# The new key and value of each sample written over the oldest row of its window while loading

## The chip, the cores and the metric

The kernel runs on one core of a Trainium2 chip. The metric is device microseconds (us) of one execution, the median of three runs; lower is better. TensorE is called PE in the rows, VectorE DVE, ScalarE ACT, GpSimd POOL and SyncE SP.

## What is computed

One step of a decoder trunk: a prompt of 512 tokens and eight samples of one new token each (`DEC_BATCH = 8`) go through a state-space head group and an attention head group, and then through one output projection. The change touches the sliding-window branch of the samples' attention. Each sample has a cache `cache_win` of the last 512 rows (a key and a value of 2 x 64 numbers each, 512 bytes), and its new token adds a 513th. The mask admits only 512 of them, so the oldest row drops out:

```python
WINDOW = 512
wrows = jnp.concatenate([cache_win[l], win_rows], axis=1)          # 513 rows
kwpos_s = past_len - win_buf + jnp.arange(win_buf + s_s)
wmask = (kwpos[None, :] <= qpos[:, None]) & (kwpos[None, :] > qpos[:, None] - WINDOW)
s = jnp.einsum('bqgrd,bwgd->bqgrw', q, kw) * scale
p = jax.nn.softmax(jnp.where(wmask[None, :, None, None, :], s, NEG_INF), axis=-1)
o_win = jnp.einsum('bqgrw,bwgd->bqgrd', p, vw)
```

The output also holds `win_sample`, the last 512 of the 513 rows.

## The kernel before

The samples are worked on in four pairs, counted 0 to 3 here. For a pair, `gather_pair` fetches the paged cache by indirect DMAs from GpSimd (tiles `kvg`, eight of 128 x 1024 numbers, 512 KB each), transposes and compresses it; `window_scores` then loads the window cache, keys into `wk` and values into `wv`, 128 partitions x 4 rows x 128 numbers for each sample, four loads in a pair, and makes the scores `Swn`; `finish_pair` does the three softmaxes, the products with the values and the gating. `finish_pair` of one pair is interleaved with `gather_pair` of the next. At the same time the prompt's attention and gated projection run: the generators `prompt` and `sample` are merged step by step, and a scheduler then sets the order of each engine. Each engine works through its own list strictly in that order.

The new token does not lie in `wk` and `wv`. `window_scores` sets the score of the oldest row (partition 0, row 0 of four) to `NEG` and adds one column, 256, for the new token, whose score `sample_setup` has made from `KN` into `snew`; `finish_pair` takes its probability out into `en`, spreads it in `pnw` over the eight samples, transposes it, and multiplies it with the new values in `kvs`:

```python
for b2 in range(2):
    for kd, t in enumerate((wk, wv)):
        nc.sync.dma_start(t[:, b2], cw[2 * pr_ + b2, :, kd].rearrange("(p r) g d -> p r (g d)", r=4))
```

`kvg`, `wk` and `wv` share four buffers (`ld`). Plain DMAs are issued from the lists of SP and ACT, and signal on eight semaphores, `DMAHW0` to `DMAHW7`, which the two engines' DMAs take in turn, in the order of the program. A DMA that takes a semaphore again has a wait in front of it for the DMA that had it before; this wait stands in the list of the engine that issues. On ACT, two such groups stand among the computing: the eight copies of `shift_window` (L1626, cache to `win_sample`, 511 KB each), four each beside two of the prompt's attention tiles, and the loads of `w_out` (L1563, L1567). On SP the transposed output of the state-space part (`yT`, four loads) and the gated projection's weights (`wg`, in halves) are loaded among the window loads.

Of the kernel before, what the change touches and what calls it, by code (L numbers as in the profile page):

```python
# [13 lines left out]
ALU = mybir.AluOpType  # L14
# [5 lines left out]
NEG = -1e30  # L20
# [16 lines left out]
def hymba_step_kernel(  # L37
# [8 lines left out]
    nc = tc.nc  # L46
    G, T = nc.gpsimd, nc.tensor
# [149 lines left out]
    p = pb("tr")  # L197
# [773 lines left out]
    for g in range(2):
        for b2 in range(2):
            V.tensor_copy(QB[64 * g:64 * g + 64, :, b2, 4 * g:4 * g + 4], qv[64 * g:64 * g + 64, :, b2, :])
    V.tensor_copy(KN.rearrange("p k b -> p (k b)"), p[:, 32:48])

    QT = [[ht("QT", 1024, F32R) for _ in range(2)] for _ in range(2)]
    KT = [[ht("KT", 1024, F32R) for _ in range(2)] for _ in range(2)]
# [294 lines left out]
            after_qk.append(lambda g=g, oT=oT: gated(g, oT))  # L1272


    snew = st([64, 8], "snew")
    gr3 = st([64, 4, 3], "gr3")
    idx = st([128, 8, 4], "idx", I32)
    ckv = cache_kv[0].rearrange("f (a j) k g d -> (f a) (j k g d)", j=2)
# [2 lines left out]
    def sample_setup():  # L1281

        pn = pb("cmp")
        for pr_ in range(4):
            for b2 in range(2):
                T.matmul(pn[32 * b2:32 * b2 + 32, 2 * pr_:2 * pr_ + 2], QB[:, pr_, b2, :], KN[:, :, 2 * pr_ + b2], start=True,
                         stop=True, skip_group_check=True, tile_position=(0, 32 * b2))
        V.tensor_copy(snew, pn[0:64, 0:8])
        pg = pb("cmp")
        for pr_ in range(4):  # L1290
            T.matmul(pg[0:64, 24 * pr_:24 * pr_ + 24], cst[:8, C_OHBT + 64 * pr_:C_OHBT + 64 * pr_ + 64], gates[:8, 4, :],
                     start=True, stop=True, skip_group_check=True)
        grow = k1("grow", 96, 64).rearrange("p (a k h) -> p a k h", k=3, h=8)
        V.tensor_tensor(grow, pg[0:64, 0:96].rearrange("p (a h k) -> p a k h", h=8, k=3),
                        cst[:64, C_OHH:C_OHH + 8].unsqueeze(1).unsqueeze(1).to_broadcast([64, 4, 3, 8]), op=ALU.mult)
        V.tensor_reduce(gr3, grow, axis=AX.X, op=ALU.add)

        with tc.issue_after(last["nr"].ins):
            for jq in range(4):
                V.tensor_scalar(idx[:, :, jq], pti, 64.0, cst[:, C_BASE:C_BASE + 1], op0=ALU.mult, op1=ALU.add)  # L1300
                if jq:
                    V.tensor_scalar(idx[:, :, jq], idx[:, :, jq], float(jq), None, op0=ALU.add)

        for kd in range(2):
            for n_ in ("h", "l"):
                XT[kd, n_] = st([128, 2, 258], "XT", F32R, tag="U", bufs=4)
                with tc.issue_after(last["nr"].ins):
                    V.memset(XT[kd, n_][:, :, 256:258].bitcast(F32), 0.0)

    def gather_pair(pr_, out):  # L1310
# [3 lines left out]
        Ssl = st([128, 513], "Ssl", bufs=2, tag="Ssl")  # L1314
        with tc.issue_after(last["nr"].ins):
            V.memset(Ssl[64:128, 512:513], NEG)
        V.tensor_copy(Ssl[0:64, 512:513], snew[:, 2 * pr_:2 * pr_ + 1])
        ph = pb("ph")
        ph3 = ph.rearrange("p (k n) -> p k n", k=2)
        kTs = []  # L1320
# [74 lines left out]
    def window_scores(pr_, out):  # L1395
        wk = ld("wk").rearrange("p (b r n) -> p b r n", b=2, r=4)
        wv = ld("wv").rearrange("p (b r n) -> p b r n", b=2, r=4)
        for b2 in range(2):
            for kd, t in enumerate((wk, wv)):
                nc.sync.dma_start(t[:, b2], cw[2 * pr_ + b2, :, kd].rearrange("(p r) g d -> p r (g d)", r=4))  # L1400
        Swn = st([128, 257], "Swn", bufs=1, tag="h0")
        kTs = []
        for b2 in range(2):
            p = pb("win")
            for r in range(4):
                T.transpose(p[:, 128 * r:128 * r + 128], wk[:, b2, r], ident)
            kT = k3("kT")
            S.copy(kT, p)
            kTs.append(kT)

        pw = pb("win")
        for a in range(2):
            for b2 in range(2):
                o = 64 * a + 32 * b2
                T.matmul(pw[o:o + 32, 0:256], QB[:, pr_, b2, :], kTs[b2][:, 256 * a:256 * a + 256], start=True, stop=True,
                         skip_group_check=True, tile_position=(0, o))
        V.tensor_copy(Swn[:, 0:256], pw[:, 0:256])
        V.memset(Swn[0:64, 0:1], NEG)
        V.memset(Swn[64:128, 256:257], NEG)
        V.tensor_copy(Swn[0:64, 256:257], snew[:, 2 * pr_ + 1:2 * pr_ + 2])  # L1420
        out[:] = [Swn, wv]
        yield 1

    def finish_pair(pr_, gat, win):
# [37 lines left out]
        for a in range(2):  # L1462
# [29 lines left out]
        V.tensor_copy(rden[:, 1:3], sm_[64:128])  # L1492
        V.tensor_tensor(rden[:, 1:3], rden[:, 1:3], sm_[0:64], op=ALU.add)

        en = st([64, 2], "en", bufs=2, tag="en")
        V.tensor_copy(en[:, 0:1], Ssl[0:64, 512:513])
        V.tensor_copy(en[:, 1:2], Swn[0:64, 256:257])
        rc = st([64, 3], "rc", bufs=2, tag="rc")
        V.reciprocal(rc, rden)
        V.tensor_tensor(rc, rc, gr3[:, pr_], op=ALU.mult)  # L1500
        V.tensor_tensor(en, en, rc[:, 1:3], op=ALU.mult)
        pnw_ = k1("pnw", 16, 64).rearrange("p (k b) -> p k b", k=2)
        V.tensor_tensor(pnw_, cst[:64, C_OHB + 8 * pr_:C_OHB + 8 * pr_ + 8].unsqueeze(1).to_broadcast([64, 2, 8]),
                        en.unsqueeze(2).to_broadcast([64, 2, 8]), op=ALU.mult)
# [253 lines left out]
```

## Time and profile before

| | us |
|---|---|
| median of three runs (467.05 to 469.04) | 468.19 |
| the profiled execution | 468.64 |
| its span, first to last instruction | 466.9 |
| PE busy | 452.1 |
| DVE busy | 348.8 |
| ACT busy | 241.3 |
| POOL busy | 95.4 |

The profile gives busy time by engine, a chain of waits followed back from the last instruction, times of single instructions on a timeline, and for chosen stretches the busy time of each engine with the granted clock of PE, the mean busy share of the core's 16 DMA engines and the GB/s they moved. Packets that overlap count twice in that share, so that it can come out over 1. A row with "q" behind the engine (SPq, ACTq) is the issue of a DMA in that engine's list. The moved bytes of one window load are 512 x 512 = 262,144.

### The profile page before, as it was taken

Reading aid. Unit: us, or ns where it says so; the run is one execution under the profiler, and the core shown is the slowest. Engines: PE = TensorE matmul, PEld = TensorE weight load, DVE = VectorE, ACT = ScalarE, POOL = GpSimd, SP = SyncE. Lnnn points to the kernel's source line nnn. Section 1 sums busy time; section 2 is a strip of 40 time slices with the busy share of each in tenths; the row PEclk is TensorE's granted clock in tenths of the full one; section 3 lists DMA queues with packets and bytes.
Section 4 is the critical chain, followed back from the end, with each engine's and each line's share of the span. In section 5 each row is a group of like instructions: output and inputs, shape, how many; then the busy total and the mean of one; then the engine's idle time right before and its main releaser. Section 6 shows DMA issues by size and latency. Waiting matters only on the chain.

```text
span 466.9 us, 10954 instructions
## 1 busy us (share of the span) xinstructions
PE 452.1 (97%) x4258; PEld 385.9 (83%) x4258; DVE 348.8 (75%) x942; ACT 241.3 (52%) x587; POOL 95.4 (20%) x104
## 2 busy tenths in 40 slices
PE   8999999999999998799999999999899999999996
PEld 4989999899999998698686776867568799799885
DVE  6978999998998998385676858687756687683332
ACT  5913764756324328475676668566856555342100
POOL 3100000056442000462342214321433010000000
PEclk9999999999999997789999999999999999999999
DMA  8776533614627433466143362429343784311211
GB/s 290 247 225 167 84 73 108 187 40 82 143 57 214 129 82 73 148 209 187 46 140 114 121 215 79 148 90 350 104 141 130 220 209 152 101 58 58 69 46 48
DMA packets 75635, 62.84 MB, mean 135 GB/s; under 512 B 29262, under 2 KB 69056, under 8 KB 75456
## 3 DMA queue, kind: packets, MB, share of 16 engines
q1 hardware_dynamic: 66208, 36.74, 28.2%
q0 software_dynamic: 4816, 17.03, 11.5%
q10 hardware_dynamic: 4560, 8.39, 5.7%
q8 instruction: 33, 0.54, 0.5%
q14 instruction: 18, 0.15, 0.1%
HBM read 55.63 MB, written 10.70 MB: 142 GB/s over the span
## 4 chain that ended last, share of the span: by engine, by line
PE 73%; DVE 13%; DMA 7%; POOL 3%; issue 2%; ACT 1%; SPq 0%; DVEq 0%; POOLq 0%; ACTq 0%
PE a L121 11%; PE a L122 11%; PE a L123 10%; PE ph L1372 8%; DMA kvg<-in_cache_kv_dram,idx 4%; PE a L1262 4%; PE t L1253 4%; PE a L1220 3%; PE t L1348 3%; PE c L1545 3%; POOL rsq L168 2%; DVE ga L62 2%; PE t L1338 2%; PE ph L473 1%; DMA x<-in_x_prompt_dram 1%
## 5 line engine op out<-in xcount | busy, mean ns | idle before, releaser
L121 PE MATMUL a<-hTh,whi 128*128 128x256 f32 (+1 forms) x192 | 54.8, 287 | 0.6 <-DVE sg L61 0.6
L122 PE MATMUL a<-hTh,wlo 128*128 128x256 f32 (+1 forms) x192 | 54.8, 287 | 0.0
L123 PE MATMUL a<-hTl,whi 128*128 128x256 f32 (+1 forms) x192 | 53.4, 284 | 0.0
L1329 POOL DMA_INDIRECT kvg<-in_cache_kv_dram,idx x32 | 32.8, 1026 | 82.2 <-PE c L1123 40.1
L168 POOL TENSOR_TENSOR rsq<-rsq,mhalf 128x6 f32<-128x6 f32 (+3 forms) x10 | 28.7, 2872 | 101.8 <-DVE rsq L62 101.8
L122 PE MATMUL a<-whi,hTl 128*128 128x256 f32 (+1 forms) x160 | 45.8, 287 | 0.0
L123 PE MATMUL a<-wlo,hTh 128*128 128x256 f32 (+1 forms) x160 | 45.3, 284 | 0.0
L121 PE MATMUL a<-whi,hTh 128*128 128x256 f32 (+1 forms) x160 | 45.2, 287 | 0.0
L1372 PE MATMUL ph<-XT,W1h 128*128 128x256 f32 x256 | 44.5, 298 | 0.0
L61 ACT ACTIVATE P<-a,mx 128x128 f32<-128x128 f32 (+3 forms) x64 | 33.6, 533 | 13.3 <-DVE mx L61 11.5
L61 DVE TENSOR_REDUCE mx<-a 128x1 f32<-128x384 f32 (+3 forms) x48 | 27.9, 596 | 13.8 <-PE a L1221 13.6
L121 PEld LDWEIGHTS a<-hTh,whi 128*128 128x128 f32 x192 | 36.2, 188 | 1.1 <-DVE sg L61 0.8
L122 PEld LDWEIGHTS a<-hTh,wlo 128*128 128x128 f32 x192 | 36.2, 188 | 0.9 <-issue 0.4
L122 PE MATMUL a<-woh,mixl 128*128 128x256 f32 x128 | 36.1, 283 | 0.0
L121 PE MATMUL a<-woh,mixh 128*128 128x256 f32 x128 | 36.1, 284 | 0.0
L123 PE MATMUL a<-wol,mixh 128*128 128x256 f32 x128 | 36.0, 283 | 0.0
L123 PEld LDWEIGHTS a<-hTl,whi 128*128 128x128 f32 x192 | 35.7, 189 | 0.1
L1372 PEld LDWEIGHTS ph<-XT,W1h 128*128 128x128 f32 x256 | 34.9, 192 | 0.3 <-ACT XT L61 0.2
L62 ACT CAST whi<-w 128x1024 fp32r<-128x1024 f32 (+4 forms) x26 | 23.9, 927 | 15.8 <-PE a L122 10.5
L61 ACT COPY pT<-t 128x512 f32<-128x512 f32 x40 | 23.1, 588 | 15.8 <-PE t L1253 12.6
L122 PEld LDWEIGHTS a<-whi,hTl 128*128 128x128 f32 x160 | 30.1, 188 | 1.2 <-issue 0.9
L121 PEld LDWEIGHTS a<-whi,hTh 128*128 128x128 f32 x160 | 29.9, 189 | 0.9 <-PE ph L473 0.4
(410 smaller groups left out, 1235.5 us busy)
## 6 DMA issues: line engine op xcount, KB each, us to landing
w<-in_w_in_dram SPq DMA_DIRECT2D x16, 512.0 KB
out_dram<-in_cache_win_dram ACTq DMA_DIRECT2D x8, 511.0 KB
x<-in_x_prompt_dram SPq DMA_DIRECT2D x4, 512.0 KB
TT<-scr_k SPq DMA_DIRECT2D x4, 512.0 KB
w<-in_w_in_dram SPq DMA_DIRECT2D x16, 128.0 KB
W1r<-in_cmp_w_dram SPq DMA_DIRECT2D x4, 512.0 KB
wk<-in_cache_win_dram SPq DMA_DIRECT2D x8, 256.0 KB
wv<-in_cache_win_dram SPq DMA_DIRECT2D x8, 256.0 KB
```

Source lines behind the costliest of these rows:

```text
L61: return f(*args, **kw)
L62: return f(*args, **kw)
L121: T.matmul(out, ah, bh, start=start, stop=False, skip_group_check=True)
L122: T.matmul(out, al, bh, start=False, stop=False, skip_group_check=True)
L123: T.matmul(out, ah, bl, start=False, stop=stop, skip_group_check=True)
L168: return G.tensor_tensor(out, out, mhalf[:parts, :cols], op=ALU.pow)
L1220: T.matmul(bank, QTv(g, r)[:, qsl], KTv(g, a)[:, brs, :n], start=(a == 0), stop=False, skip_group_check=True)
L1253: T.transpose(p[:, 128 * r:128 * r + 128], P[r][:, br, 128 * kt:128 * kt + 128], ident)
L1262: mm = T.matmul(po[64 * br:64 * br + 64, :], kvt[kt - 1][:, c0:c0 + 64], behind[kt - 1][br][0], start=(kt == 1), stop=(kt == i + 1), tile_ ...
L1329: G.indirect_dma_start(out=gt_, out_offset=None, in_=ckv, in_offset=bass.IndirectOffsetOnAxis(ap=idx[:, 2 * pr_ + b2, jq:jq + 1], axis=0))
L1348: T.transpose(p[:, 256 * g + 128 * b2:256 * g + 128 * b2 + 128], gts[jq][b2][:, o:o + 128], ident)
L1372: T.matmul(ph3[:, kd], (W1l if part == 1 else W1h)[kd][a][:, wsl], (xl if part == 2 else xh)[:, e, a:a + 256], start=(jq == 0 and kd == 0 ...
```

## The change

The new key and value go into `wk` and `wv` in place of the oldest row. Each of the four loads of a pair becomes three DMAs on SP: partitions 1 to 127 from the cache, rows 1 to 3 of partition 0 from the cache, and the new row from `kvs` (in SBUF) to row 0 of partition 0. `Swn` has 256 columns; the masked column, the extra column, the second half of `KN`, `snew`, `en` and `pnw`, and the second product with `kvs` are gone.

```diff
     def window_scores(pr_, out):
...
         for b2 in range(2):
+            b = 2 * pr_ + b2
             for kd, t in enumerate((wk, wv)):
-                nc.sync.dma_start(t[:, b2], cw[2 * pr_ + b2, :, kd].rearrange("(p r) g d -> p r (g d)", r=4))
-        Swn = st([128, 257], "Swn", bufs=1, tag="h0")
+                src = cw[b, :, kd].rearrange("(p r) g d -> p r (g d)", r=4)
+                nc.sync.dma_start(t[1:128, b2], src[1:128])
+                nc.sync.dma_start(t[0:1, b2, 1:4], src[0:1, 1:4])
+                nc.sync.dma_start(t[0:1, b2, 0], kvs[b:b + 1, 512 + 128 * kd:640 + 128 * kd])
+        Swn = st([128, 256], "Swn", bufs=1, tag="h0")
...
-        V.tensor_copy(Swn[:, 0:256], pw[:, 0:256])
-        V.memset(Swn[0:64, 0:1], NEG)
-        V.memset(Swn[64:128, 256:257], NEG)
-        V.tensor_copy(Swn[0:64, 256:257], snew[:, 2 * pr_ + 1:2 * pr_ + 2])
+        V.tensor_copy(Swn, pw[:, 0:256])
...
-        en = st([64, 2], "en", bufs=2, tag="en")
-        V.tensor_copy(en[:, 0:1], Ssl[0:64, 512:513])
-        V.tensor_copy(en[:, 1:2], Swn[0:64, 256:257])
+        en = st([64, 1], "en", bufs=2, tag="en")
...
-        V.tensor_tensor(en, en, rc[:, 1:3], op=ALU.mult)
+        V.tensor_tensor(en, Ssl[0:64, 512:513], rc[:, 1:2], op=ALU.mult)
...
-        for kd in range(2):
-            T.transpose(p[0:8, 320 + 64 * kd:384 + 64 * kd], pnw_[:, kd], i64)
+        T.transpose(p[0:8, 320:384], pnw_, i64)
...
-            for kd in range(2):
-                c0, o = 384 + 256 * kd, 320 + 64 * kd + 32 * b2
-                todo[2 * b2 + 1].append((pT1[0:8, o:o + 32], kvs[:, c0:c0 + 128]))
+            o = 320 + 32 * b2
+            todo[2 * b2 + 1].append((pT1[0:8, o:o + 32], kvs[:, 384:512]))
```

Three places in the order of the built programs follow: each row is line, operation, written tile, read tile, size, and the semaphores that it waits for.

On SP, before, the window loads of pair 0 (`wk_3499`, `wv_3500`) and of pair 1 (`wk_4234`, `wv_4235`):

```order
L1400 DMA wk_3499<-in_cache_win_dram 128x4x128 [waits DMASW1_49,DMASW5_49,DVE_49,DMAHW1_49,PE_49,Pool_49]
L1400 DMA wv_3500<-in_cache_win_dram 128x4x128 [waits DMASW2_49,DMASW6_49,DVE_49,DMAHW2_49,PE_49,Pool_49]
L1400 DMA wk_3499<-in_cache_win_dram 128x4x128 [waits DMAHW3_49]
L1400 DMA wv_3500<-in_cache_win_dram 128x4x128 [waits DMAHW4_49]
L1400 DMA wk_4234<-in_cache_win_dram 128x4x128 [waits DMASW7_49,DMAHW1_49,DMASW2_49,DMAHW3_49,DVE_49,DMAHW5_49,PE_49,Pool_49]
L1400 DMA wk_4234<-in_cache_win_dram 128x4x128 [waits DMAHW6_49]
L1400 DMA wv_4235<-in_cache_win_dram 128x4x128 [waits DMASW3_49,DMASW5_49,DMASW0_49,DMAHW7_49,DVE_49,PE_49]
L1400 DMA wv_4235<-in_cache_win_dram 128x4x128 [waits DMAHW0_49]
```

On SP, after, the loads of pair 1 alone (`wk_4233`, `wv_4234`):

```order
L1402 DMA wk_4233<-in_cache_win_dram 127x4x128 [waits DMAHW0_49,DMAHW1_49,DMASW7_49,DMAHW5_49,DMASW2_49,DMAHW7_49,DVE_49,PE_49]
L1403 DMA wk_4233<-in_cache_win_dram 1x3x128 [waits DMAHW6_49]
L1404 DMA wk_4233<-kvs 1x16x8
L1402 DMA wk_4233<-in_cache_win_dram 127x4x128
L1403 DMA wk_4233<-in_cache_win_dram 1x3x128
L1404 DMA wk_4233<-kvs 1x16x8 [waits DMAHW2_49]
L1402 DMA wv_4234<-in_cache_win_dram 127x4x128 [waits DMASW3_49,DMASW5_49,DMASW0_49,DMAHW3_49,DVE_49,PE_49]
L1403 DMA wv_4234<-in_cache_win_dram 1x3x128 [waits DMAHW4_49]
L1404 DMA wv_4234<-kvs 1x16x8 [waits DMAHW5_49]
L1402 DMA wv_4234<-in_cache_win_dram 127x4x128 [waits DMAHW7_49]
L1403 DMA wv_4234<-in_cache_win_dram 1x3x128 [waits DMAHW1_49]
L1404 DMA wv_4234<-kvs 1x16x8 [waits DMAHW3_49]
```

Four rows have become twelve, the size of the large one is 127x4x128 in place of 128x4x128, and the first eight of them take the semaphores DMAHW5, 6, 7, 0, 1, 2, 3 and 4.

On ACT, before, the first four copies of `shift_window`, which the scheduler puts beside pair 1:

```order
L61 COPY oT_4004<-a_3931 128x512 [waits PE_49]
L1626 DMA out_dram<-in_cache_win_dram 16x8176 [waits DMAHW1_49]
L61 CAST XT_2787<-t_3989 128x2x256 [waits PE_49]
L1626 DMA out_dram<-in_cache_win_dram 16x8176 [waits DMAHW2_49]
L61 CAST XT_2791<-t_4130 128x2x256 [waits PE_49]
L1626 DMA out_dram<-in_cache_win_dram 16x8176 [waits DMAHW3_49]
L61 ACTIVATE P_4042,den_4010<-a_4037,mx_4031 128x384 [waits DVE_49]
L61 COPY fT_3896<-c_3946 128x512 [waits PE_49]
L1626 DMA out_dram<-in_cache_win_dram 16x8176 [waits DMAHW4_49]
```

On ACT, after, the same four:

```order
L61 COPY oT_4006<-a_3933 128x512 [waits PE_49,Activation_49]
L1622 DMA out_dram<-in_cache_win_dram 16x8176 [waits DMAHW6_49]
L61 CAST XT_2786<-t_3991 128x2x256 [waits PE_49]
L1622 DMA out_dram<-in_cache_win_dram 16x8176 [waits DMAHW0_49]
L61 CAST XT_2790<-t_4129 128x2x256 [waits PE_49]
L61 COPY fT_3899<-c_4047 128x320 [waits PE_49]
L1622 DMA out_dram<-in_cache_win_dram 16x8176 [waits DMAHW2_49]
L61 ACTIVATE P_4044,den_4012<-a_4039,mx_4033 128x384 [waits DVE_49]
L61 ACTIVATE P_4073,den_4012<-a_4063,mx_4062 128x384 [waits DVE_49]
L1622 DMA out_dram<-in_cache_win_dram 16x8176 [waits DMAHW4_49]
```

Before, DMAHW1 to DMAHW4 had last been taken by the loads of pair 0. After, DMAHW6, 0, 2 and 4 have last been taken by rows 2, 4, 6 and 8 of the SP rows above, the loads of pair 1 itself.

On SP, before, from the values of pair 2 (`wv_4943`) to the first weights of the gated projection:

```order
L1400 DMA wv_4943<-in_cache_win_dram 128x4x128 x2
L1016 DMA yT_4851<-scr_y 128x520
L1016 DMA yT_4857<-scr_y 128x520
L1016 DMA yT_4861<-scr_y 128x520
L1016 DMA yT_4867<-scr_y 128x520
L1027 DMA wg_5176<-in_w_glu_dram 128x4x128 x2
```

On SP, after, the same stretch, with the waits:

```order
L1402 DMA wv_4942<-in_cache_win_dram 127x4x128 [waits DMASW3_49,DMASW4_49,DMASW1_49,DMASW5_49,DMASW0_49,DMASW6_49,DVE_49,DMAHW4_49,PE_49,Pool_49]
L1403 DMA wv_4942<-in_cache_win_dram 1x3x128 [waits DMAHW6_49]
L1404 DMA wv_4942<-kvs 1x16x8 [waits DMAHW0_49]
L1015 DMA yT_4850<-scr_y 128x520 [waits DMAHW2_49,PE_49,Activation_49]
L1015 DMA yT_4856<-scr_y 128x520 [waits DVE_49,PE_49,DMAHW3_49,Activation_49,Pool_49]
L1015 DMA yT_4860<-scr_y 128x520 [waits DMAHW4_49,PE_49,Activation_49]
L1015 DMA yT_4866<-scr_y 128x520 [waits DMAHW5_49,PE_49,Activation_49]
L1402 DMA wv_4942<-in_cache_win_dram 127x4x128 [waits DMAHW6_49]
```

The second load of these values now stands behind the `yT` loads, and the third `yT` load takes DMAHW4, which the first row here took. Beside pair 2 the four copies of ACT take DMAHW3, 5, 7 and 1 in the same way, the last of them behind the second load of `wk`. In pair 3 the `w_out` loads of ACT take semaphores of that pair's loads; the last that does so, the second half of `wo_6146`, takes the one of the last load of `wv`.

## Rows read from the trace of the kernel before

**Rows 1.** The page's head, and busy time, share and instructions by engine.

```profile
span 466.9 us, 10954 instructions
PE 452.1 (97%) x4258; PEld 385.9 (83%) x4258; DVE 348.8 (75%) x942; ACT 241.3 (52%) x587; POOL 95.4 (20%) x104
```

**Rows 2.** The page's chain that ended last, share of the span by engine.

```profile
PE 73%; DVE 13%; DMA 7%; POOL 3%; issue 2%; ACT 1%; SPq 0%; DVEq 0%; POOLq 0%; ACTq 0%
```

**Rows 3.** The page's DMA issues: out<-in, engine, count, KB each.

```profile
out_dram<-in_cache_win_dram ACTq DMA_DIRECT2D x8, 511.0 KB
...
wk<-in_cache_win_dram SPq DMA_DIRECT2D x8, 256.0 KB
```

**Rows 4.** Timeline of SP: start us, us, line, transfer; first issues of the four pairs.

```profile
210.44 0.62 SPq L1400 DMA_DIRECT2D wk<-in_cache_win_dram  x1
...
252.56 1.22 SPq L1400 DMA_DIRECT2D wk<-in_cache_win_dram  x2
...
307.10 1.21 SPq L1400 DMA_DIRECT2D wk<-in_cache_win_dram  x2
...
361.20 1.22 SPq L1400 DMA_DIRECT2D wk<-in_cache_win_dram  x2
```

**Rows 5.** Stretches: us, busy by engine (instructions), clock, DMA share, GB/s.

```profile
211.00:211.80 0.80, 0.80 (x9) 0.80 (x8) 0.80 (x2) 0.09 (x1) 0.40 (x1) 1.00 0.00 0
211.80:212.20 0.40, 0.40 (x6) 0.40 (x5) 0.40 (x3) 0.40 (x1) 0.00 (x0) 1.00 0.49 148
212.00:216.25 4.25, 4.25 (x38) 4.16 (x38) 3.75 (x10) 2.85 (x12) 0.24 (x1) 1.00 0.82 244
366.00:367.00 1.00, 1.00 (x11) 0.97 (x9) 0.93 (x3) 0.59 (x1) 0.39 (x1) 1.00 1.14 339
```

**Rows 6.** Timeline of PE: second transposes of the keys, pairs 0 and 1.

```profile
227.09 0.60 PE L1406 MATMUL c<-cst,wk 128*128 128x128 f32 x4
...
280.18 0.60 PE L1406 MATMUL c<-cst,wk 128*128 128x128 f32 x4
```

**Rows 7.** Timeline of ACT: copies, `yT` casts, a `wg` cast, `w_out` loads.

```profile
267.64 0.73 ACTq L1626 DMA_DIRECT2D out_dram<-in_cache_win_dram  x1
...
317.43 0.52 ACTq L1626 DMA_DIRECT2D out_dram<-in_cache_win_dram  x1
...
327.40 0.63 ACT L62 CAST yTh<-yT 128x520 fp32r<-128x520 f32 x1 [2.50 <-DMA yT<-scr_y]
...
328.09 1.28 ACT L62 CAST yTh<-yT 128x520 fp32r<-128x520 f32 x2
...
385.04 1.05 ACT L62 CAST wgh<-wg 128x1024 fp32r<-128x1024 f32 x1
...
393.91 1.30 ACTq L1567 DMA_DIRECT2D wo<-in_w_out_dram  x2
```

**Rows 8.** Timeline of POOL: two of the indirect loads.

```profile
252.87 0.98 POOL L1329 DMA_INDIRECT kvg<-in_cache_kv_dram,idx  x1 [3.85 <-DVE xr L62]
...
264.11 0.98 POOL L1329 DMA_INDIRECT kvg<-in_cache_kv_dram,idx  x1 [3.74 <-DVE rc L62]
```

**Rows 9.** One more stretch, columns as in the fifth group.

```profile
194.50:201.30 6.80, 5.06 (x30) 4.88 (x31) 3.30 (x8) 3.47 (x12) 4.46 (x6) 0.50 0.78 259
```

**Rows 10.** By tile or line: operation, count, ns min/median/max, first and last start.

```profile
L62 DVE MEMSET Swn<- x8: 59/59/59, 165.1 to 404.5; 64x1 f32 x8
L62 DVE COPY Swn<-snew x4: 135/146/146, 182.6 to 378.6; 64x1 f32<-64x1 f32 x4
L62 DVE COPY en<-Swn x4: 145/145/145, 262.5 to 421.5; 64x1 f32<-64x1 f32 x4
L1524 PE MATMUL c<-cst,pnw x8: 216/216/217, 271.4 to 427.2; 64*8 64x64 f32 x8
L1545 PE MATMUL c<-kvs,fT x32: 267/268/293, 275.4 to 432.8; 8*32 8x128 f32 x32
```

**Rows 11.** Timeline of PE: the products with the values of the last pair.

```profile
431.00 0.62 PE L1545 MATMUL c<-wv,fT 128*32 128x128 f32 x16
```

More of the change, by code (lines that the diff above doesn't have):

```diff
@@ L961, in hymba_step_kernel @@
     V.memset(QB, 0.0)
-    KN = st([128, 2, 8], "KN")
+    KN = st([128, 8], "KN")
     p = pb("tr")
@@ L967, in hymba_step_kernel @@
         T.transpose(p[:, 8 * r:8 * r + 8], qsv[:, r].rearrange("p g d -> p (g d)"), ident[:8, :8])
-    for kd in range(2):
-        T.transpose(p[:, 32 + 8 * kd:40 + 8 * kd], kvs[:, 256 * (kd + 1):256 * (kd + 1) + 128], ident[:8, :8])
+    T.transpose(p[:, 32:40], kvs[:, 256:384], ident[:8, :8])
     qv = p[:, 0:32].rearrange("p (r a b) -> p a b r", r=4, b=2)
@@ L973, in hymba_step_kernel @@
             V.tensor_copy(QB[64 * g:64 * g + 64, :, b2, 4 * g:4 * g + 4], qv[64 * g:64 * g + 64, :, b2, :])
-    V.tensor_copy(KN.rearrange("p k b -> p (k b)"), p[:, 32:48])
+    V.tensor_copy(KN, p[:, 32:40])
     QT = [[ht("QT", 1024, F32R) for _ in range(2)] for _ in range(2)]
@@ L1272, in attention @@
             after_qk.append(lambda g=g, oT=oT: gated(g, oT))
-    snew = st([64, 8], "snew")
+    snew = st([64, 4], "snew")
     gr3 = st([64, 4, 3], "gr3")
@@ L1285, in sample_setup @@
             for b2 in range(2):
-                T.matmul(pn[32 * b2:32 * b2 + 32, 2 * pr_:2 * pr_ + 2], QB[:, pr_, b2, :], KN[:, :, 2 * pr_ + b2], start=True,
+                T.matmul(pn[32 * b2:32 * b2 + 32, pr_:pr_ + 1], QB[:, pr_, b2, :], KN[:, 2 * pr_ + b2:2 * pr_ + b2 + 1], start=True,
                          stop=True, skip_group_check=True, tile_position=(0, 32 * b2))
-        V.tensor_copy(snew, pn[0:64, 0:8])
+        V.tensor_copy(snew, pn[0:64, 0:4])
         pg = pb("cmp")
@@ L1316, in gather_pair @@
             V.memset(Ssl[64:128, 512:513], NEG)
-        V.tensor_copy(Ssl[0:64, 512:513], snew[:, 2 * pr_:2 * pr_ + 1])
+        V.tensor_copy(Ssl[0:64, 512:513], snew[:, pr_:pr_ + 1])
         ph = pb("ph")
@@ L1500, in finish_pair @@
         V.tensor_tensor(rc, rc, gr3[:, pr_], op=ALU.mult)
-        V.tensor_tensor(en, en, rc[:, 1:3], op=ALU.mult)
-        pnw_ = k1("pnw", 16, 64).rearrange("p (k b) -> p k b", k=2)
-        V.tensor_tensor(pnw_, cst[:64, C_OHB + 8 * pr_:C_OHB + 8 * pr_ + 8].unsqueeze(1).to_broadcast([64, 2, 8]),
-                        en.unsqueeze(2).to_broadcast([64, 2, 8]), op=ALU.mult)
+        V.tensor_tensor(en, Ssl[0:64, 512:513], rc[:, 1:2], op=ALU.mult)
+        pnw_ = k1("pnw", 8, 64)
+        V.tensor_scalar(pnw_, cst[:64, C_OHB + 8 * pr_:C_OHB + 8 * pr_ + 8], en, None, op0=ALU.mult)
         V.tensor_scalar(Pc2, Pc2, rc[:, 0:1], None, op0=ALU.mult)
@@ L1508, in finish_pair @@
         V.tensor_scalar(Ssl[:, 0:512], Ssl[:, 0:512], sm_[:, 0:1], None, op0=ALU.mult)
-        S.mul(Swn[:, 0:256], Swn[:, 0:256], sm_[:, 1:2])
+        S.mul(Swn, Swn, sm_[:, 1:2])
         i64 = ident[:64, :64]
@@ L1522, in finish_pair @@
         T.transpose(p[:, 256:320], Pc2, i64)
-        for kd in range(2):
-            T.transpose(p[0:8, 320 + 64 * kd:384 + 64 * kd], pnw_[:, kd], i64)
+        T.transpose(p[0:8, 320:384], pnw_, i64)
         S.copy(pT1[:, 0:320], p[:, 0:320])
-        V.tensor_copy(pT1[0:8, 320:448], p[0:8, 320:448])
+        V.tensor_copy(pT1[0:8, 320:384], p[0:8, 320:384])
         yield 1
@@ L1538, in finish_pair @@
             todo[2 * b2].append((pT1[:, 256 + 32 * b2:288 + 32 * b2], vc))
-            for kd in range(2):
-                c0, o = 384 + 256 * kd, 320 + 64 * kd + 32 * b2
-                todo[2 * b2 + 1].append((pT1[0:8, o:o + 32], kvs[:, c0:c0 + 128]))
-        for j in range(8):
+            o = 320 + 32 * b2
+            todo[2 * b2 + 1].append((pT1[0:8, o:o + 32], kvs[:, 384:512]))
+        for j in range(7):
             for q in range(4):
```

## The prediction

> **What bounds the kernel now.** I read the page's head and busy line first [rows 1]: PE is busy 452.1 of 466.9 us, 97%, so it has almost no idle time in which a late transfer could hide, and any stop of PE shows in the span nearly whole. The chain of waits says the same [rows 2]: PE 73%, DVE 13%, DMA 7%. Then I looked for the slack of the work that changes. The list of DMA issues gives eight loads of `wk`, and as many of `wv`, at 256 KB, and eight copies of 511 KB from ACT [rows 3]. SP issues the first load of the pairs at 210.44, 252.56, 307.10 and 361.20 [rows 4]. In pair 0 PE transposes the second half of the keys, which is the third load of the pair, from 227.09 on [rows 6]: these loads now have 16.65 us from issue to use and never hold PE.
>
> **The new loads: how many engines carry one.** In the order of the built program other transfers stand in 16 equal parts: a copy of 511 rows is 16x8176, one key row is 1x16x8. The large load stands as 127x4x128, and 127 has no divisor but 1. So either it goes whole to one of the 16 DMA engines, or the engines share it as they share 128 rows. I take the first, because the cut into 16 parts has a purpose only if transfers are dealt out by equal parts of their outer dimension; no row of this trace shows such a load.
>
> A rule bears on this. The Trainium skill ("DMA: Bandwidth & Descriptors", section "Why a DMA increments its semaphore by 16 and not by 1") says that a DMA from SP or ACT uses the largest number of engines up to 16 that divides the slowest dimension of both sides, and gives 127 partitions as an example of one engine; by it the sum is the 597 below, without it about 468. No run here shows it yet.
>
> **Price of one load.** It moves 127 x 4 x 512 = 260,096 bytes. The fastest stretch I found moves 339 GB/s over 16 engines, 21.2 each; while the four loads of pair 0 run, 244 GB/s at a share of 0.82, so 244 / (0.82 x 16) = 18.6 for a busy engine [rows 5]. That gives 12.3 to 14.0 us, and I take 13.1 (19.9 GB/s). Spread, it would take about 260,096 / 339 GB/s = 0.8 us; that is the other end. The same page, section "Specifications", states about 27 GiB/s for an engine; by it a load would take 9.0 us and the sum below would be about 544, an estimate from a figure that the stretches above don't reach.
>
> Two smaller prices belong to it. First bytes move about 1.4 us after an issue (210.44 to 211.8: no bytes until then, 148 GB/s after) [rows 4, 5]. And every other transfer puts a sixteenth on the same engine, at 19.9 GB/s 1.64 us for 512 KB and 0.82 for 256 KB. The 1x3x128 and 1x16x8 pieces move 1.5 KB and 512 bytes; I set them at nothing. The eight further issues of a pair cost SP 0.61 us each [rows 4], 4.9 us, which lies under the 13.1 us of the load before; if the loads were spread, the third load would be issued four issues, 2.5 us, later, and the cushion of 16.65 us still covers that.
>
> **Who waits.** Four loads are now 52 us on one engine, and what waits differs by pair. I go through them; "late" is against the trace of before, and adds up, since nothing in PE's list can run ahead of a stopped transpose for long.
>
> Pair 0. PE wants the third load at 227.1. It ends at 210.4 + 1.4 + 3 x 13.1 + 3.3 (two indirect loads of 512 KB that fall beside, as at 252.87 [rows 8]) = 254.4. Late: 27.3. The engine is free of the fourth at 267.5.
>
> Pair 1. First issue 252.6 + 27.3 = 279.9, so the backlog is gone. PE itself would wait for the second load of `wk`, but ACT is stopped sooner: by the order, its fourth copy of `shift_window` waits for DMAHW4, which now belongs to the 1x3x128 piece behind the third large load (it belonged to pair 0 before), and everything behind it in ACT's list (casts, exponentials, PSUM copies) that PE needs waits too. Before, that copy was issued at 267.64 [rows 7]. Now the load ends at 279.9 + 1.4 + 39.3 + 3.3 + 3 x 1.64 (the three copies ahead) = 328.8. Late: 61.2. Engine free at 343.5.
>
> Pair 2. First issue 307.1 + 61.2 = 368.3. The fourth copy, at 317.43 before [rows 7], here waits for the second `wk` load: 402.4 against 378.6. Then the third `yT` load, which stands on SP behind the third large load and takes its DMAHW4, waits for that: 368.3 + 1.4 + 39.3 + 3.3 + 6.6 (four copies) = 418.9, and lands some 2.2 us later (1.4 and 0.8 for 266 KB), 421.1. Its cast on ACT began at about 328.75 (the second of the two from 328.09 [rows 7]; the first, at 327.40, had waited 2.50 us for its `yT`, so there is no slack). Late: 92.4.
>
> Pair 3. First issue 361.2 + 92.4 = 453.6. The `w_out` loads on ACT wait for this pair's loads in turn, the last of them for the fourth: 453.6 + 1.4 + 4 x 13.1 + 1.6 (a gather) + 3.3 (four halves of `wg`) + 9.8 (`w_out` loads: six of 256, three of 512 KB) = 522.1. It was issued at about 394.6 (second of the two from 393.91 [rows 7]). Late: 127.5.
>
> **The sum.** 466.9 + 127.5 = 594.4. Three small terms. After a long stop PE may run at half clock for a while: 6.8 us at a granted 0.50 stand in the trace once [rows 9], which costs 3.4; after four stops 0 to +14, I take +7, half. PE can work ahead of ACT at the last stop, whose products with the values come at 431.0, well behind 394.6 [rows 7, 11]: 0 to -13, I take -5. The removed work: four transposes of 216 ns, sixteen products that pipeline like those with the values (0.62 us for sixteen [rows 11]; 268 ns is their latency), eight memsets of 59, and four copies each of 146 and 145 ns [rows 10], together 0.9 + 0.6 + 0.5 + 1.2 = 3.2 us if all were on the path; most DVE work has slack, so -1 (0 to -3.2). Span 595.4; the execution is 1.7 us longer than the span now (468.64 against 466.9), so **597 us**. The profiled time is 0.1% from the median, and I leave it there. Everything but the price of a load is small: it enters 13 times (3 + 3 + 3 + 4), so 12.3 or 14.0 us make 587 or 609, and the small terms widen that to about 570 to 622. As the price is of a case no row shows, I reach further: 540 is a price of 8.7 us, 650 one of 17.2.
>
> **Rivals.**
>
> Spread after all: the large load is shared by the engines, takes under 1 us as today, and the whole change is three more small DMAs behind each and the removed work: 468, bounds -3 to +2. For it: the trace of before shows only spread loads, at 244 GB/s [rows 5]. Against it: the cut into 16 elsewhere.
>
> ACT is not held: loads on one engine, but ACT's waits for the shared semaphores end with the small pieces or earlier ones, and only true readers wait. Pair 0 as above, 27.3. Pair 1: second `wk` load at 279.9 + 1.4 + 26.2 + 1.6 + 6.6 = 315.7 against 280.18 [rows 6], 35.5. Pair 2: the `yT` load as above, from an issue of max(307.1 + 35.5, 343.6): 393.2, landed 395.4, 66.7. Pair 3: issue 427.9, the last half of `wg` at 460.4 against 385.04 + 66.7 = 451.7 [rows 7], 75.4; the last load of `wv` is in by 496, before 431.0 + 75.4 [rows 11]. Together 466.9 + 75.4 + 1.7 + some 1 = 545. For it: no row shows which of two waits on ACT ends last. Against it: the order names the semaphores, and a list is worked through strictly in order.
>
> Faster: loads spread or hidden, and the removed work all on the path: 3.2 us of PE's and DVE's chain, 465.5. It decides only if over 2.3 us of the 3.2 count, and DVE, with 348.8 of 466.9 busy [rows 1], has slack over most of the span.
>
> **How the numbers follow.** One engine with all stops: 0.82. One engine with ACT free: 0.07. Spread, no difference: 0.07. Faster: 0.04. A measurement of this kernel tells about 0.5% from no change, so faster 0.04, same 0.07, slower 0.89. The range 540 to 650 takes in the main case with its price from 8.7 to 17.2 us and the second rival; about 0.15 stays outside, nearly all of it at 468 and below.
>
> **What would show it.** In the changed kernel's trace: from the first issue of a pair, a stretch of about 50 us with a DMA share near 1/16 and about 20 GB/s, where the four loads took 4.25 us before; PE idle by about 27 us before the second key transposes of pair 0; ACT idle in front of a copy of `shift_window` in pair 1 and of the `w_out` loads in pair 3, and before a `yT` cast in pair 2; SP's issues in a run of twelve. If the first stretch shows 200 GB/s or more, the forecast is wrong at its first step. If it shows 20 GB/s and the time is near 545, the waits on ACT are the wrong step; if the stops are where I put them with other lengths, the price is.

## The result, and the profile after

The changed kernel takes 589.45 us (median of six runs, 584.69 to 590.76) against 468.66 for the kernel before in the same comparison: 1.257 times as long, 95% interval 1.253 to 1.261. The forecast was 597, with 540 to 650 as its range.

The page of the kernel after: its head, busy time by engine, and the chain of waits by engine and by line, to be read against [rows 1, 2].

```profile
span 586.9 us, 10944 instructions
PE 477.5 (81%) x4237; PEld 402.7 (69%) x4237; DVE 346.8 (59%) x922; ACT 241.2 (41%) x587; POOL 93.9 (16%) x104
...
PE 44%; SPq 24%; DMA 16%; DVE 10%; issue 2%; POOL 2%; ACT 1%; ACTq 0%; POOLq 0%; DVEq 0%
```

The span is 120.0 us longer. PE falls from 97% to 81% busy, and a quarter of the chain that ended last is now SP issuing DMAs, which had 0% before [rows 2].

The same view as in [rows 5] (busy by engine, PE clock, DMA share, GB/s), between the second and the fourth load of pair 0:

```profile
228.50:252.00 23.50, 2.88 (x12) 2.10 (x10) 2.62 (x7) 0.81 (x4) 0.76 (x1) 0.57 0.07 22
...
238.00:248.00 10.00, 0.00 (x0) 0.00 (x0) 0.00 (x0) 0.00 (x0) 0.00 (x0) 0.50 0.07 22
```

This is the stretch that the prediction asked for first. The DMA share is 0.07, about one engine of 16, at 22 GB/s, where the four loads had moved at 244 [rows 5]. The trace's packets of 512 bytes, one for each row, pass one after the other, about 43 in a microsecond. In the ten microseconds from 238 on no engine computes at all.

SP's timeline of pair 0 (start us, us, line, transfer), the first issues of the three other pairs, the held issue and the `yT` loads of pair 2, and the last load of pair 3, beside [rows 4]:

```profile
209.68 0.74 SPq L1402 DMA_DIRECT2D wk<-in_cache_win_dram  x1
210.47 13.88 SPq L1403 DMA_DIRECT2D wk<-in_cache_win_dram  x1
224.40 0.60 SPq L1404 DMA_DIRECT2D wk<-kvs  x1
225.24 0.71 SPq L1402 DMA_DIRECT2D wv<-in_cache_win_dram  x1
226.00 10.69 SPq L1403 DMA_DIRECT2D wv<-in_cache_win_dram  x1
...
237.33 0.69 SPq L1402 DMA_DIRECT2D wk<-in_cache_win_dram  x1
238.06 10.56 SPq L1403 DMA_DIRECT2D wk<-in_cache_win_dram  x1
...
280.39 0.68 SPq L1402 DMA_DIRECT2D wk<-in_cache_win_dram  x1
...
362.91 0.68 SPq L1402 DMA_DIRECT2D wk<-in_cache_win_dram  x1
...
393.95 11.46 SPq L1403 DMA_DIRECT2D wv<-in_cache_win_dram  x1
...
406.13 4.00 SPq L1015 DMA_DIRECT2D yT<-scr_y  x4
...
445.43 0.72 SPq L1402 DMA_DIRECT2D wk<-in_cache_win_dram  x1
...
494.41 0.69 SPq L1402 DMA_DIRECT2D wv<-in_cache_win_dram  x1
495.14 16.66 SPq L1403 DMA_DIRECT2D wv<-in_cache_win_dram  x1
```

One thing here was not foreseen: the issue behind a large load (L1403, the 1x3x128 piece) takes 10.56 to 16.66 us, where an issue took 0.62 before [rows 4]. SP is held until about three quarters of the large load have gone. More on that in the last section.

PE and ACT at the places where the prediction put the four stops (start, duration, and in brackets the idle time before and what ended it); before, they are [rows 6, 7]:

```profile
252.23 1.09 PE L1410 MATMUL c<-cst,wk 128*128 128x128 f32 x4 [20.85 <-DMA wk<-kvs]
...
311.74 0.59 ACT L61 CAST XT<-t 128x512 fp32r<-128x512 f32 x1 [13.99 <-DMA wk<-in_cache_win_dram]
...
327.14 0.52 ACTq L1622 DMA_DIRECT2D out_dram<-in_cache_win_dram  x1
327.70 0.58 ACT L61 ACTIVATE P<-a,mx 128x384 f32<-128x384 f32 x1 [13.92 <-DMA wv<-in_cache_win_dram]
...
411.04 1.30 ACT L62 CAST yTh<-yT 128x520 fp32r<-128x520 f32 x2 [8.71 <-DMA yT<-scr_y]
412.40 1.26 ACT L62 CAST yTh<-yT 128x520 fp32r<-128x520 f32 x2
...
515.58 0.66 ACTq L1563 DMA_DIRECT2D wo<-in_w_out_dram  x1
516.29 0.63 ACT L62 ACTIVATE gx<-gx 128x512 f32<-128x512 f32 x1 [5.36 <-DMA wv<-in_cache_win_dram]
```

In pair 0 PE waits 20.85 us for the third load (and 3.30 for the first); what lands last of it is the new row, which SP could issue only behind the held issue. In pair 1 it is ACT: the operation at 327.70 neither reads nor writes `wv`, yet the view gives a `wv` load as what ended the idle time. Between the two stands the fourth copy of `shift_window`, and that is what waited, for the semaphore that the 1x3x128 piece behind the third large load had taken. In pair 2 ACT waits before the first `yT` cast, in pair 3 in front of the `w_out` loads.

### The profile page after: what moved, and what is told of

The parts are those of the page before. It is cut to its first block, busy times and chain, and to the rows that moved or that the text cites. A ratio compares the mean times of both kernels' runs of the same rounds, so it can differ in the third digit from the quotient of the medians.

```text
span 586.9 us, 10944 instructions
## 1 busy us (share of the span) xinstructions
PE 477.5 (81%) x4237; PEld 402.7 (69%) x4237; DVE 346.8 (59%) x922; ACT 241.2 (41%) x587; POOL 93.9 (16%) x104
## 4 chain that ended last, share of the span: by engine, by line
PE 44%; SPq 24%; DMA 16%; DVE 10%; issue 2%; POOL 2%; ACT 1%; ACTq 0%; POOLq 0%; DVEq 0%
SPq L1403 21%; PE a L121 7%; PE a L122 7%; PE a L123 7%; DMA wv<-in_cache_win_dram 7%; DMA wk<-in_cache_win_dram 3%; PE ph L1371 3%; PE a L1261 2%; PE a L1219 2%; POOL rsq L168 2%; PE t L1252 2%; DMA kvg<-in_cache_kv_dram,idx 2%; DVE ga L62 1%; PE t L1347 1%; SPq L1402 1%
## 5 line engine op out<-in xcount | busy, mean ns | idle before, releaser
L1371 PE MATMUL ph<-XT,W1h 128*128 128x256 f32 x256 | 50.3, 324 | 22.6 <-ACT XT L61 22.6
L61 DVE TENSOR_TENSOR XT<-t,XT 128x512 fp32r<-128x512 f32 x32 | 21.9, 686 | 62.3 <-ACT XT L61 62.2
L1371 PEld LDWEIGHTS ph<-XT,W1h 128*128 128x128 f32 x256 | 39.3, 214 | 24.4 <-ACT XT L61 23.7
L1219 PE MATMUL a<-KT,QT 128*128 128x512 f32 (+2 forms) x96 | 31.9, 431 | 15.7 <-ACT P L61 15.7
L61 ACT CAST XT<-t 128x512 fp32r<-128x512 f32 x32 | 18.6, 589 | 52.4 <-DMA wk<-in_cache_win_dram 26.7
```

Of the source, the lines that this page charges most:

```text
L61: return f(*args, **kw)
L1219: T.matmul(bank, QTv(g, r)[:, qsl], KTv(g, a)[:, brs, :n], start=(a == 0), stop=False, skip_group_check=True)
L1371: T.matmul(ph3[:, kd], (W1l if part == 1 else W1h)[kd][a][:, wsl], (xl if part == 2 else xh)[:, e, a:a + 256], start=(jq == 0 and kd == 0 ...
```

## The experiments

Each is one edit of the kernel after (of the kernel before in `e2_before_split`). The question was which part of the change costs the 121 us, whether it is the count of partitions, and whether the stops hang on semaphores.

**The 127-partition piece alone, in the kernel before** (`e2_before_split`):

```diff
-                nc.sync.dma_start(t[:, b2], cw[2 * pr_ + b2, :, kd].rearrange("(p r) g d -> p r (g d)", r=4))
+                src = cw[2 * pr_ + b2, :, kd].rearrange("(p r) g d -> p r (g d)", r=4)
+                nc.sync.dma_start(t[1:128, b2], src[1:128])
+                nc.sync.dma_start(t[0:1, b2], src[0:1])
```

> The kernel before with one part of the change alone: each window load is split into partitions 1 to 127 and partition 0, both from the cache; the extra score column, mask and second product stay, and no new row is written. Theory: all of the loss comes from the 127-partition piece: 560 to 592, four loads of 11.5 to 13 us in a row at about 22 GB/s in each pair. As eight DMAs per pair in place of twelve share the eight semaphores otherwise, the stop of pair 1 is some 12 us shorter (ACT's last copy waits for the second load), that of pair 2 some 12 us longer (the yT loads stand behind four). Rival (the cost sits in the new row out of SBUF, or in the taken-out work): 466 to 472.

Measured: 589.39 us, ratio 1.257 (1.253 to 1.261), as slow as the whole change. Its window row during pair 0, ACT's last copy of the first four, and the `yT` casts:

```profile
232.00:250.00 18.00, 1.24 (x4) 0.55 (x3) 2.20 (x6) 0.81 (x4) 0.77 (x1) 0.50 0.07 22
...
314.38 1.16 ACTq L1628 DMA_DIRECT2D out_dram<-in_cache_win_dram  x2
...
421.87 1.28 ACT L62 CAST yTh<-yT 128x520 fp32r<-128x520 f32 x2 [21.13 <-DMA yT<-scr_y]
423.22 0.63 ACT L62 CAST yTh<-yT 128x520 fp32r<-128x520 f32 x1
```

Again 22 GB/s at a share of 0.07. Pair 1 begins at 283.08 here, so ACT's stop ends some 32 us after the first issue (the last of the two issues from 314.38; 46.8 in the kernel after); pair 2 begins at 361.51, and the third `yT` cast, at 423.22, comes 62 us later (49.5). That is the shift of about a load each way that the semaphores and SP's order gave. The new row and the removed work have no part in the loss. This kernel still has one DMA more for each load than the kernel before; whether that counts, the third experiment shows.

**All 128 partitions, and the new row written over the old one** (`e1_full_then_row`):

```diff
-                nc.sync.dma_start(t[1:128, b2], src[1:128])
-                nc.sync.dma_start(t[0:1, b2, 1:4], src[0:1, 1:4])
-                nc.sync.dma_start(t[0:1, b2, 0], kvs[b:b + 1, 512 + 128 * kd:640 + 128 * kd])
+                nc.sync.dma_start(t[:, b2], src)
+        for b2 in range(2):
+            b = 2 * pr_ + b2
+            for kd, t in enumerate((wk, wv)):
+                nc.sync.dma_start(t[0:1, b2, 0], kvs[b:b + 1, 512 + 128 * kd:640 + 128 * kd])
```

> The changed kernel, but each load takes all 128 partitions x 4 rows from the cache again (four DMAs), and four DMAs of one row each then write the new key and value over the oldest row. Theory (one DMA engine carries the 127-partition load): with 128 partitions the loads are as short as before, the overwriting rows wait for them inside the 16.65 us cushion, and only the removed work is left: 465.5 to 468.5, 0 to 3 us under before; DMA at over 200 GB/s behind a pair's first issue. Rival (the new row itself, its DMAs and the waits between load and row, are the cost): still well over 500, since the rows are written here too and now wait for the load.

Measured: 467.76 us, ratio 0.999 (0.996 to 1.002). The window row behind the first issue of pair 0 (208.14 in this trace):

```profile
211.00:213.00 2.00, 2.00 (x20) 2.00 (x18) 1.81 (x5) 1.60 (x7) 0.00 (x0) 1.00 1.00 300
```

300 GB/s with PE busy throughout, and the whole loss is gone. The waits of the new rows for the loads lie in the cushion.

**127 cut into 112 and 15** (`e3_112_15`, and `e11_112_15_again`, the same kernel measured again):

```diff
-                nc.sync.dma_start(t[1:128, b2], src[1:128])
+                nc.sync.dma_start(t[1:113, b2], src[1:113])
+                nc.sync.dma_start(t[113:128, b2], src[113:128])
```

> The changed kernel with the 127 partitions cut into 112 (1 to 112) and 15 (113 to 127), both beginning off partition 0 as before the cut; sixteen DMAs per pair. Theory (the engines used are given by a divisor of the partitions): 112 goes to 16 engines and 15 to 15, and a pair's loads take 4 to 6 us: 464 to 472. Rival (a load that begins at partition 1, or that leaves out a row, is what is slow): as the changed kernel, 575 to 592. Rival (twelve or sixteen issues per pair on SP are the cost): as slow or slower than the changed kernel.

> e3_112_15 once more (112 and 15 partitions, no DMA waits for another one's data), beside e10 and e12. Theory: 465 to 468, ratio to before 0.994 to 1.000 as the first time. Rival (the first difference was noise): 468 to 469.5.

Measured: 466.98 us, ratio 0.997 (0.994 to 0.9995), and again 467.07 us, 0.997 (0.995 to 0.999). The window row over the first load of 112 partitions in pair 0 of `e3_112_15`:

```profile
211.10:211.60 0.50, 0.50 (x7) 0.46 (x6) 0.50 (x3) 0.12 (x1) 0.00 (x0) 1.00 0.99 298
```

All sixteen engines are busy. The same rows go to the same places from the same odd starting partition, with four more DMAs in a pair, and nothing is lost. Neither the start at partition 1 nor the issues on SP is the cause; the count 127 is. The piece of 15 also tells which rule holds: by the largest power of two in the count, 127, 122 and 112 would fall on one, two and sixteen engines too, but 15 on one. Its 60 packets pass in about half a microsecond, up to 23 in a tenth of one, where one engine passes about 43 in a whole one: 15 goes to several engines, as the divisor says.

**127 cut into 122 and 5** (`e4_122_5`; the diff is that above with 123 in place of 113):

> The changed kernel with the 127 partitions cut into 122 (2 x 61) and 5. Theory (largest divisor up to 16): 122 goes to two engines, 5 to five; a load takes 122 x 2048 / 2 bytes at 21 to 22 GB/s, about 5.8 us, and DMA runs at 40 to 45 GB/s in the stretch where the changed kernel showed 22. The stops shrink from 120 us to some 25 (third load of pair 0 about 231 against 227.1, then +9, +6 and +6): 478 to 505. Rival (only multiples of 16 or 8 are spread, everything else goes to one engine): 560 to 590 and 22 GB/s. Rival (one engine only for a prime count): 464 to 472.

Measured: 511.46 us, ratio 1.092 (1.089 to 1.096). Its window row in pair 0, and SP from the third load to the fourth:

```profile
226.00:232.00 6.00, 0.10 (x1) 0.00 (x0) 2.12 (x6) 0.53 (x4) 0.76 (x1) 0.94 0.13 40
...
225.17 0.71 SPq L1402 DMA_DIRECT2D wk<-in_cache_win_dram  x1
225.92 4.22 SPq L1403 DMA_DIRECT2D wk<-in_cache_win_dram  x1
230.19 0.69 SPq L1404 DMA_DIRECT2D wk<-in_cache_win_dram  x1
230.93 0.58 SPq L1405 DMA_DIRECT2D wk<-kvs  x1
231.56 0.70 SPq L1402 DMA_DIRECT2D wv<-in_cache_win_dram  x1
```

The share is 0.13, two engines of 16, at 40 GB/s: so the large load does go to as many engines as the divisor says. The time was 6 us above what I had given for it. From one large load to the next SP needs 6.4 us (225.17 to 231.56: the held issue and three more in line), not the 5.8 of the bytes alone; that the stops add this up to the 6 us is my reading and was not tested.

**A quarter of each load on 127 partitions** (`e9_quarter_on_127`):

```diff
-                nc.sync.dma_start(t[1:128, b2], src[1:128])
-                nc.sync.dma_start(t[0:1, b2, 1:4], src[0:1, 1:4])
+                nc.sync.dma_start(t[:, b2, 1:4], src[:, 1:4])
+                nc.sync.dma_start(t[1:128, b2, 0], src[1:128, 0])
```

> The changed kernel with a quarter of each load on 127 partitions: rows 1 to 3 of all 128 partitions in one DMA, row 0 of partitions 1 to 127 in a second, the new row in a third; the semaphores fall as in the changed kernel, twelve DMAs per pair. Theory (one engine for the 127): 127 x 512 bytes at 21.5 GB/s are 3.0 us, with the large part some 3.6 us a load; third load of pair 0 about 222 against 227.1, no stop; third load of pair 1 some 20 us after the first issue where 15 were free, so a stop of 2 to 6; little after: 468 to 478. Next issue on SP held for less than 2 us. Rival (a fixed price of each 127-partition DMA or of the new row, whatever its size): 560 and more.

Measured: 478.15 us, ratio 1.021 (1.013 to 1.028), just over the upper edge. SP's third load of pair 0 to the fourth, PE's second key transposes, and ACT's fourth copy:

```profile
217.53 0.59 SPq L1402 DMA_DIRECT2D wk<-in_cache_win_dram  x1
218.16 0.36 SPq L1403 DMA_DIRECT2D wk<-in_cache_win_dram  x1
218.57 3.63 SPq L1404 DMA_DIRECT2D wk<-kvs  x1
222.24 0.59 SPq L1402 DMA_DIRECT2D wv<-in_cache_win_dram  x1
...
228.21 0.60 PE L1410 MATMUL c<-cst,wk 128*128 128x128 f32 x4
...
273.22 0.52 ACTq L1622 DMA_DIRECT2D out_dram<-in_cache_win_dram  x1
```

The price falls with the bytes: with a quarter of them on one engine, 4.7 us from load to load beside indirect loads, PE does not wait in pair 0, and ACT's copy comes 5.6 us later than before [rows 7] instead of 59.5. Two per cent remain; I read them as shorter stops of the same kind (two `yT` casts of pair 2 wait 2.68 and 2.27 us, where one had waited 2.50 [rows 7]). Of the 9.7 us of span, 7.2 lie between the first issues of pairs 2 and 3; what makes them up was not tested. SP's issue was held longer than the 2 us I had expected.

**The same DMAs in another order** (`e7_small_first`): the 1x3x128 piece and the new row ahead of the 127 partitions.

> The changed kernel with each load's three DMAs in another order: the 1x3x128 piece, the new row, then the 127 partitions. Every transfer and every reader is the same; what moves is which DMA has which semaphore. Theory (ACT and SP are stopped by semaphores that the loads have taken): ACT's fourth copy in pair 1 now waits for the row ahead of the third large load, so that stop falls from 46.8 us after the pair's first issue to some 30 (two loads), the last w_out load waits for three loads in place of four, and the other two stops stay: 550 to 572. Rival (only the readers of the loaded tiles and the queue of the one engine count): as the changed kernel, 583 to 592.

Measured: 574.01 us, ratio 1.227 (1.218 to 1.236), two microseconds over my range. ACT at the fourth copy of pair 1 (whose first issue is at 280.86), and at the last `w_out` load that waits for pair 3 (first issue 443.22):

```profile
314.89 0.58 ACT L61 ACTIVATE P<-a,mx 128x384 f32<-128x384 f32 x1 [16.04 <-DMA wk<-in_cache_win_dram]
315.00 0.52 ACTq L1622 DMA_DIRECT2D out_dram<-in_cache_win_dram  x1
...
500.46 0.61 ACTq L1563 DMA_DIRECT2D wo<-in_w_out_dram  x1
```

The two stops are 34.1 and 57.2 us long, where the kernel after has 46.8 and 70.2: each about one load shorter, though every transfer and every reader is the same. So ACT was held by semaphores, which the rival "ACT is not held" denied. Of these 25.5 us only 15 show in the time: from the end of the stop in pair 1 to the next first issue (358.65) it is now 43.7 us, 35.8 in the kernel after, where 19 of the matmuls of that stretch had run during the longer stop.

**The large DMAs issued by GpSimd** (`e6_large_from_pool`: `nc.gpsimd` in place of `nc.sync` in the line of the 127 partitions).

> The changed kernel with only the 127-partition DMAs issued by GpSimd, the other two of a load by SP. The semaphores of SP and ACT are then no longer taken by the large loads. Theory in the sharper form of the Trainium skill (page DMA: Bandwidth & Descriptors, section Why a DMA increments its semaphore by 16 and not by 1: GpSimd's direct copies may be cut into ceil(partitions / 16) per engine): loads on all engines, over 150 GB/s behind the first issue, 465 to 475, with POOL's list a few us busier. Rival (one engine whoever issues): about 22 GB/s, pair 0 as late as in the changed kernel, the semaphore stops gone, GpSimd's indirect loads behind the window loads on that engine: 540 to 580.

Measured: 584.80 us, ratio 1.251 (1.242 to 1.260). Its window rows while one load moves and while mostly two do, POOL's issue of one, and PE behind it:

```profile
228.00:232.00 4.00, 4.00 (x35) 3.82 (x36) 1.92 (x5) 3.58 (x16) 2.97 (x1) 1.00 0.08 23
...
238.00:244.00 6.00, 0.00 (x0) 0.00 (x0) 0.00 (x0) 0.00 (x0) 0.00 (x0) 0.58 0.21 38
...
226.43 4.54 POOL L1402 DMA_DIRECT2D wv<-in_cache_win_dram  x1 [8.90 <-issue]
...
254.57 0.66 PE L1337 MATMUL t<-cst,kvg 128*128 128x128 f32 x2 [20.53 <-DMA kvg<-in_cache_kv_dram,idx]
```

Each load still goes to one engine: one alone moves 23 GB/s at a share of 0.08, and its packets, now 63 of 4096 bytes and one of 2048, pass one after the other, mostly 194 ns each. Two in flight move up to 43 GB/s, so they are on different engines. About half of the share of 0.21 comes from packets of 32 bytes, 945 for each load, which carry none of its bytes. So the rival has the mechanism, but neither the time (5 us over its range) nor pair 0, where with two loads side by side the second key transposes begin at 233.08 with next to no wait. The Trainium skill ("DMA: Bandwidth & Descriptors", section "Why a DMA increments its semaphore by 16 and not by 1") gives for some direct copies from GpSimd a spread by ceil(partitions / 16); these loads did not get it. An issue takes 4.5 us of POOL, and PE now waits for the indirect loads behind them.

**The price of the new rows, and what the removed work is worth.** `e10_two_rows` is `e1_full_then_row` with the rows of both samples in one DMA (`t[0:1, :, 0]` from `kvs[2 * pr_:2 * pr_ + 2, ...]`); `e12_no_new_row` takes those two lines out as well.

> As e1_full_then_row, but the new rows of both samples of a pair go in one DMA for keys and one for values (six DMAs per pair in place of eight). Theory: the loads are hidden, what is left is the removed work: 464.5 to 468, up to 3 us under before. Rival (the waits of the new rows for the loads cost as much as the removed work gives): 468 to 470.

> Loads of 128 partitions as in the kernel before and no new row at all, so that the samples' new key and value are left out of the window branch and the oldest row stays in: the removed work of the change alone, without any DMA that it adds. Theory (the removed work is worth 0 to 3.2 us, of which 1): 465 to 468.5. Rival (it lies beside other work): 468 to 469.5. A time well under e10 and e11 would show a price of the new rows.

Measured: 467.81 us, ratio 0.997 (0.994 to 0.9995), and 467.81 us, ratio 0.999 (0.996 to 1.001). In the same comparison the kernel before had 469.25. The new rows have no price that shows. The versions with spread loads lie 0.1 to 0.3% under the kernel before, 0.5 to 1.5 us, which agrees with the 1 us (0 to 3.2) of the sum without proving its size. `e3_112_15`, in both measurements, and `e10_two_rows` lie 0.3% under it with intervals that just leave out 1.

## Why the prediction was right, step by step

**One engine: shown.** 22 GB/s at a share of 0.07 and one packet after the other, two engines' worth with 122 partitions, spread with 112 and 15. The rule of the Trainium skill ("DMA: Bandwidth & Descriptors", section "Why a DMA increments its semaphore by 16 and not by 1") agrees with the traces for the loads that SP issues: 127 to one engine, 122 to two, 112 to sixteen, 15 to several.

**Where it stops: right in all four pairs; what holds it, in three.** In pair 2 the prediction named the third `yT` load, by its semaphore. That wait is there, 2.1 us on SP, but ACT had stood since the first `yT` cast, 8.71 us to 411.04, because SP, held behind the third large load, issued the first `yT` load only at 406.13. The third cast then began at 412.40 without a wait. The place and nearly the length are the same, and a held issue on SP was not in the prediction. From a pair's first issue to the end of its stop, and the stretches between, in us:

| | before | forecast | measured |
|---|---|---|---|
| pair 0, to the second key transposes | 16.7 | 44.0 | 42.6 (209.68 to 252.23) |
| pair 1, to ACT's fourth copy | 15.1 | 48.9 | 46.8 (280.39 to 327.14) |
| pair 2, to the third `yT` cast | 21.6 | 52.8 | 49.5 (362.91 to 412.40) |
| pair 3, to the last waiting `w_out` load | 33.4 | 68.5 | 70.2 (445.43 to 515.58) |
| sum of the four | 86.8 | 214.2 | 208.9 |
| the rest of the span | 380.1 | 381.2 | 378.0 |
| span | 466.9 | 595.4 | 586.9 |

The stops add 122 us where 127 were forecast, and the rest is 2 us shorter where 1 us more was.

**The price of a load: about a tenth too high, and partly made up by luck.** 260,096 bytes at the measured 22 GB/s are 11.8 us; I had taken 13.1, and the 12.3 that I gave as the lower end, from the fastest stretch found, was no floor either. A single engine with nothing but this load to do ran faster than any engine's share of the busy stretches of [rows 5]. With 11.8 the same four sums would be 40.1, 45.0, 48.9 and 63.3; measured are 2.5, 1.8, 0.6 and 6.9 us more. So the loads were given 17 us too much and what else holds the engine and SP between them 12 us too little; that the one makes up most of the other is luck. The Trainium skill ("DMA: Bandwidth & Descriptors", section "Specifications") states about 27 GiB/s for an engine. The 9.0 us that the prediction estimated from this figure are 2.8 us short of the measured price.

**Pair 3: longer than forecast** by 1.7 us, although the price was lower. In it the third load is issued only at 480.37, 4 us after SP was free of the hold of the second at 476.31; I had taken the four loads as one unbroken row. Whether that gap makes up the 6.9 us I have not tested.

**The small terms.** I had +7 for PE at half clock after the stops and -5 for work done ahead. The stretches between the stops show them: against before, +2.7 behind pair 0 (252.23 to 280.39), -3.7 behind pair 1, +0.6 behind pair 2, -1.0 at the end, and the first issue comes 0.8 earlier. That net hides two larger parts. The same stretches of the kernel after, with the granted clock third from the end of each row:

```profile
252.23:280.39 28.16, 27.58 (x171) 18.75 (x172) 15.26 (x41) 15.55 (x47) 8.96 (x13) 0.82 0.33 102
327.14:362.91 35.77, 34.25 (x246) 26.34 (x248) 23.97 (x62) 23.16 (x59) 10.97 (x14) 0.90 0.31 96
412.40:445.43 33.03, 32.86 (x230) 23.70 (x230) 22.11 (x47) 21.95 (x49) 11.57 (x15) 0.94 0.40 120
515.58:586.90 71.32, 66.24 (x582) 58.87 (x582) 32.42 (x78) 12.74 (x26) 0.00 (x0) 0.95 0.22 71
```

PE is granted 1.00 there before. These clocks are some 27 us at half speed, which by the prediction's own count, half of it, would cost 13.5 us, the upper end of its 0 to +14 (the trace of before has two stretches at 0.50, from 180.9 and from 194.5, not one). Against this, 109 more matmuls than before ran inside the four stops, most of them in pair 1, so that fewer were left behind them. By this count both terms were set too small, and they nearly cancel; no run separates them. PE's busy time rose by 25.4 us with 21 matmuls fewer: 28.2 more inside the stops, where PE had time, and 2.9 less outside.

**The rivals.** "Spread after all" and "faster" fell with the first row of the trace. "ACT is not held" gave 545 (546 with the 343.6 that it names for pair 2, where the sum goes on from 342.6); the kernel took 589, and moving the semaphores alone moved the stops.

## What to carry to other kernels

Before a load is trimmed by one partition, look at what the new count divides by: here 127 partitions in place of 128 made a load of about 1 us into one of 12 and a hidden load into the bound, while 112 + 15, or a full load with one row written over it, cost nothing. A DMA that has become slow holds more than its readers: look for every later DMA that takes its semaphore, and for what stands behind those in the lists of other engines. And read a stop's "released by" with the issue rows beside it: an operation that seems to wait for a tile it never touches stands behind a DMA issue that does.

## What had not been expected of the hardware

An issue on SP is held when much is still queued on one DMA engine. Behind a load of 508 packets of 512 bytes on one engine the next issue took 10.56 to 16.66 us; with 122 partitions, 244 packets on each of two engines, 2.6 to 8.8; with 127 packets it grew through pair 0 of `e9_quarter_on_127` from 1.40 to 3.92, and was up to 9.26 in pair 1; with loads over sixteen engines an issue took 0.5 to 0.6 in pair 0 of `e1_full_then_row`. Where the hold ends can be counted in the packets, taken in the order of issue: in the twelve holds of pairs 0 to 2 of the kernel after, 111 to 121 of the 508 were left; in the four of pair 0 with 122 partitions, some 108 to 118 on each of the two engines. By the table above it changed the sum little; that what SP had to issue would have stood behind the load on the same engine anyway is argued, not tested.

GpSimd's issue of a direct load with 127 partitions took 4.54 to 4.63 us each, and two copies on DVE beside the first two of them took 8.73 us together, where two such copies took 0.75 in the kernel before (at 211.83); whether one caused the other was not tested:

```profile
208.54 8.73 DVE L62 COPY xr<-kvg 128x512 f32<-128x512 f32 x2
217.20 0.40 DVE L62 TENSOR_REDUCE mxc<-pcs 128x8 f32<-128x256 f32 x1
...
L1402 POOL DMA_DIRECT2D wk<-in_cache_win_dram x8: 4579/4602/4632, 207.8 to 455.8; - x8
```
